# One transfer per load for a pair's keys and low-rank inputs, token rows of v stored by head, token rows of b and k by TensorE transposes

## The chip, the cores and the metric

The kernel runs on one core of one Trainium2 chip. The metric is device time in microseconds (us) of that core, from one launch; lower is better. The kernel before takes 3005.72 us, the median of 3 runs (3000.78 to 3016.42).

## What is computed

One layer of a hybrid diffusion backbone on 1024 latent tokens and 128 context tokens, with a model width of 1024, all in fp32. A combined input projection (`z = h @ w_in`) feeds a bidirectional RWKV-7 mixer of 16 heads x 64 and a gated short convolution. Both are projected, merged by gates and added to x. A gated MLP with a width-3 convolution follows. The part that the change touches is the RWKV-7 mixer:

```python
def step(s, inp):
    r_t, w_t, k_t, v_t, a_t, b_t = inp           # a = -kk, b = kk * a
    sa = jnp.einsum('bhij,bhj->bhi', s, a_t)
    s = s * w_t[:, :, None, :] + sa[..., None] * b_t[:, :, None, :] + v_t[..., None] * k_t[:, :, None, :]
    return s, jnp.einsum('bhij,bhj->bhi', s, r_t)
...
w_log = -softplus(-(decay_w0[d] + tanh(wdown) @ decay_w2[d])) - 0.5
decay = exp(-exp(w_log))
a = sigmoid(iclr_a0[d] + adown @ iclr_a2[d])
k_d = heads(k * (1.0 + (a - 1.0) * k_a))
y, s_fin = wkv_scan(s0, rh, heads(decay), k_d, vh, kk, heads(a), reverse)
```

It is run forward and backward over the tokens.

## The kernel before, in words

**Two kinds of work on TensorE.** `Kern.dense` (line 230) goes through a list of jobs, each one 128-column tile of a projection: 3 column blocks (`th`) of 384 tokens x 8 contraction tiles x 3 matmuls (fp32 split in a high and a low part). Into this stream, `step_streams` (line 151) weaves the mixer's own small matmuls. The weaving is planned in Python while the program is built: each instruction adds a cost in ns to a clock, a stream goes on when the clock has passed its due time `s.t` and its condition holds, and priorities are handed to the scheduler of the language below. TensorE, ScalarE, VectorE and the DMA queue of SyncE (SP) each work their instructions in order. `K.dma` (line 125) sends nearly all transfers to the SP queue; only `Xw` goes to ScalarE's and `Dm` to GpSimd's.

**Dense jobs of this part, in order** (lines 553 to 695): two low-rank inputs (`T_WD`, `T_AD`, written by `lora_evac` to the DRAM tiles `LO`), then k, r and v of pair 0 and of pair 1 (`rkv`), the gate input `T_GD`, the gate output `gjobs` (24 fp32 matmul tiles from `gts`, evacuated by `g_evac` on ScalarE and stored to `GS`), then `rkv` of the other pairs between the convolution's jobs, the 16 gate jobs, and the 8 jobs of `w_pb`. A pair is 2 heads (128 channels). `gts` are 3 tiles of the tag `rot`, which has 4 buffers; `k_evac` takes its tile `kt` from the same tag.

**Streams of the mixer** (class `Scan`, line 984):
- `prep` (line 1106), 24 times (8 pairs x 3 blocks): loads k, kk and r of the pair (3 transfers into `krk`), the low-rank inputs by `lora_in` (2 transfers into `llo`, 49 calls), and writes for both directions the features FA (a, r times decay) and FB (b and k over decay) to DRAM, one transfer each per segment.
- `features` and `prep2` (lines 1190, 1208), 36 items (4 groups of 2 pairs x 9 chunks of 128 tokens): load FA into `E` and `O` and FB into `BK` (one buffer), form the Gram matrices `gpb` and `gpk`, and turn b and k into token rows: for each of 8 blocks, 2 heads and b or k, one matmul of `BK` against the identity into `bps` (lines 1243 to 1246), 32 matmuls of 64x64 for an item.
- `vfill` (line 1252): brings the token rows of v into `Wt`, 4 transfers for each half of an item. The rows were made by `v_evac` (transposes `vps`, line 599) and stored to `VT[d]`.
- `chain`, `merge`, `scan`, `finish`: a triangular inverse on VectorE (31 steps), then the state recurrence on TensorE, then the normalisation and the store `oa`.

Of the kernel before, what the change touches and what calls it, by code (L numbers as in the profile page):

```python
# [15 lines left out]
P = 128  # L16
# [325 lines left out]
def build(tc, ins, outs, dbg=None):  # L342
# [4 lines left out]
    with es:  # L347
# [9 lines left out]
        dt_ = lambda name, shape=(P, T): dr.tile(list(shape), F32, name=name, tag=name)  # L357
        RS = [dt_(f"rs{m}") for m in range(8)]
        KS = [dt_(f"ks{m}") for m in range(8)]
        KKS = [dt_(f"kks{m}") for m in range(8)]  # L360
        VS = [dt_(f"vs{m}") for m in range(8)]
        LO = [dt_(f"lo{m}") for m in range(4)]
        FA = [dt_(f"fa{m}", (P, 2, 2, 2 * T)) for m in range(4)]
        FB = [dt_(f"fb{m}", (P, 2, 2, 2 * T)) for m in range(4)]
        BS = [dt_(f"bs{m}") for m in range(8)]
        VT = [dt_(f"vt{d}", (T, D)) for d in range(2)]
        GS = [dt_(f"gs{m}") for m in range(8)]
# [142 lines left out]
        with ExitStack() as ea:  # L510
# [16 lines left out]
            K.sc = Scan(K, const, apool, par, pc, mask, ident, bones, x0, hw0, hka, oka,  # L527
                        dict(RS=RS, KS=KS, KKS=KKS, VS=VS, LO=LO, GS=GS, OA=OA, FA=FA, FB=FB, BS=BS, VT=VT))
            hx = lambda k: (H[k][0], H[k][1])
# [9 lines left out]
            def lora_evac(base, func):  # L539
                def ev(s, th, ps):  # L540
                    sl = slice(th * TH, th * TH + TH)
                    z = st.tile([P, TH], F32, name="lz", tag="st")
                    K.act(s, z, ps, func)
                    hi = st.tile([P, TH], F32R, name="lh", tag="st")
                    lo = st.tile([P, TH], F32R, name="ll", tag="st")
                    K.act(s, hi, z, AF.Copy)
                    K.tt(s, lo, z, hi.bitcast(F32), ALU.subtract)
                    for d in range(2):
                        K.dma(LO[base + d][0:64, sl], hi[64 * d:64 * d + 64, :].bitcast(F32), "lo")
                        K.dma(LO[base + d][64:128, sl], lo[64 * d:64 * d + 64, :].bitcast(F32), "lo")  # L550
                return ev

            job(T_WD, lora_evac(0, AF.Tanh))
            job(T_AD, lora_evac(2, AF.Copy))

# [9 lines left out]
            def g_evac(s, m, th, ps):  # L565
                z = st.tile([P, TH], F32, name="gz", tag="st")
                K.act(s, z, ps, AF.Copy)
                K.dma(GS[m][:, th * TH:th * TH + TH], z, "gs")
# [13 lines left out]
            def v_evac(m):  # L582

                def ev(s, th, ps):
# [8 lines left out]
                    def post(s2):  # L593
                        t0, ms = th * TH, slice(m * P, m * P + P)
                        for d, zd in enumerate((z, zr)):
                            yield
                            pv = K.psd.tile([P, 512], F32, name="vps", tag="psd")
                            for j in range(3):
                                K.transp(pv[:, j * P:j * P + P], zd[:, j * P:j * P + P], ident, cost=110)
                            s2.t = clk.now  # L600
                            zt = st.tile([P, 3, P], F32, name="vt", tag="st")
                            K.act(s2, zt, pv[:, :TH].rearrange("p (j f) -> p j f", f=P), AF.Copy)
                            for a, b, _ in latctx(th):
                                r0 = t0 + a if d == 0 or t0 + a >= TL else TL - t0 - b
                                K.dma(VT[d][r0:r0 + b - a, ms].rearrange("(j t) f -> t j f", t=P),
                                      zt[:, a // P:b // P], "vt")
                        K.events.add(("v", m, th))
# [76 lines left out]

            rkv(0)
            rkv(1)
            job(T_GD, gd_evac)
            gjobs()
# [295 lines left out]
class Scan:  # L984
# [4 lines left out]
    def __init__(self, K, const, apool, par, pc, mask, ident, bones, x0, hw0, hka, oka, dr):  # L989
# [25 lines left out]
        self.W = self.one.tile([P, 2, 4, 2, C], F32, name="Wt", tag="Wt")  # L1015
        self.y, self.PC = {}, {}
        self.NY = 4

    def start(self):
# [4 lines left out]
        def prep_all(s):  # L1024
            yield lambda: ("kk", 0, 0) in ev and ("r", 0, 0) in ev
            self.lora_in(0, 0)
            for p in range(NPAIR):
                yield lambda: ("kk", p, 0) in ev and ("r", p, 0) in ev
                yield from self.lora_w(s, p)
                for th in (0, 2, 1):  # L1030
                    yield lambda: ("kk", p, th) in ev and ("r", p, th) in ev
                    yield from self.prep(s, p, th)
                    ev.add(("prep", p, th))

        def ready(i, what):
            pp, n = self.items[i]
            ths = {n // 3, (7 - n) // 3} if n < 8 else {2}
            return all((what, 2 * pp + q, th) in ev for q in range(2) for th in ths)

# [66 lines left out]
    def prep(self, s, p, th):  # L1106
# [6 lines left out]
        krk = self.one.tile([P, 3, TH], F32, name="krk", tag="krk")  # L1113
        for j, src in enumerate((dr["KS"], dr["KKS"], dr["RS"])):
            K.dma(krk[:, j, :], src[p][:, t0:t0 + TH], "ld")
        if pp not in self.PC:
# [5 lines left out]
        for d in range(2):  # L1122
# [52 lines left out]
            for a, b in segs:  # L1175
                g0 = t0 + a if d == 0 or t0 + a >= TL else TL - t0 - b
                K.act(s, PC[:, q, d, g0 // C:(g0 + b - a) // C], e65[:, a // C:b // C, C], AF.Copy)
                for dst, src in (("FA", FAo), ("FB", B)):
                    K.dma(dr[dst][pp][:, q, d, 2 * g0:2 * (g0 + b - a)],
                          src[:, a // C:b // C].rearrange("p c a t -> p (c a t)"), "fa")  # L1180
            yield

    def lora_in(self, th, d):

        llo = self.one.tile([P, 2, TH], F32R, name="llo", tag="llo")
        for w in range(2):
            self.K.dma(llo[:, w, :].bitcast(F32), self.dr["LO"][2 * w + d][:, th * TH:th * TH + TH], "llo")
        self.llo = llo, self.K.clk.now + 4000
# [19 lines left out]
    def prep2(self, s, i, pp, n):  # L1208
# [5 lines left out]
        for q in range(2):  # L1214
# [4 lines left out]
            for e in range(4 * q, 4 * q + 4):  # L1219
                for ps, a in ((gb, 1), (gk, 0)):  # L1220
                    for h in range(2):
                        o = HS[h if a else 1 - h]
                        calls.append(lambda ps=ps, a=a, h=h, e=e, o=o: K.mm(
                            ps[o, e - 4 * q, :], BK[HS[h], e, a, :], (E, O)[h][HS[h], e, :], True, True, 85))
            K.group(calls)
# [12 lines left out]
        for x in range(4):  # L1238
            for c in range(2):
# [3 lines left out]
        pv = [self.psm.tile([P, 512], F32, name="bps", tag="psm").rearrange("p (e t) -> p e t", t=C) for _ in range(2)]  # L1243
        K.group([lambda e=e, a=a, h=h: K.mm(pv[h][HS[h if a else 1 - h], e, :], BK[HS[h], e, a, :],
                                            self.ident[HS[h], HS[h]], True, True, 45)
                 for e in range(8)[::-1] for a in range(2) for h in range(2)])
        s.t = K.clk.now
# [4 lines left out]
    def vfill(self, s, i, pp, n):  # L1252
# [5 lines left out]
        for c in range(2):  # L1258
# [8 lines left out]
            ch = (2 * n + c if n < 8 else c) * C  # L1267
            for d in range(2):
                rows = self.dr["VT"][d][base + ch:base + ch + C, 256 * pp:256 * pp + 256]
                rows = rows.rearrange("t (q h f) -> t q h f", q=2, h=2)  # L1270
                for h in range(2):
                    K.dma(Wt[64 - 64 * h:128 - 64 * h, h, d::2, c, :], rows[:, :, h, :], "v")
            if c == 0 and n == 8:
# [259 lines left out]
```

## Time and profile before

| | us |
|---|---|
| median of 3 runs (lowest, highest) | 3005.72 (3000.78, 3016.42) |
| profiled execution, its own time | 2994.76 |
| its span, first to last instruction | 2993.0 |
| TensorE busy in the span | 2771.6 |
| VectorE busy | 2009.7 |
| ScalarE busy | 1266.4 |

The span is nearly all of the execution's time. PE is TensorE's matmul row, PEld its weight loads (which overlap the matmuls), DVE VectorE, ACT ScalarE, POOL GpSimd, SP the queue of SyncE that issues transfers. Matmuls are pipelined, so a busy PE is not a PE at its peak. "The granted clock" is the share of full speed that TensorE was given; in the rows it is either full or half, and a stretch's number is the mean. A name such as `psd<-gz,wraw` is the output tile and then the inputs.

### The profile page before, as it was taken

The page shows a single profiled execution, that of the slowest core. Times are in us where ns is not written, and L with a number is a line of the kernel's source. Part 1 is how long each engine was busy: PE and PEld are TensorE (multiplying, and loading weights), DVE is VectorE, ACT ScalarE, POOL GpSimd, SP SyncE. Part 2 cuts the span into 40 slices and gives each one's busy share as a digit, 9 for nine tenths or more (in the row PEclk, how much of TensorE's full clock was granted, in tenths as well). Part 3 has the DMA queues.
Part 4 walks back from the last instruction along what each step waited for, and adds up shares of the span by engine and source line. Part 5 has one row for each costly group of instructions (what it writes and reads, how often), then busy time and mean ns, then how long its engine had stood idle before and what let it go on. Part 6 is the DMA issues. An engine that isn't in the chain of part 4 may idle for free. (4 is left out here: it accounts for less than half of the span.)

```text
span 2993.0 us, 63336 instructions
## 1 busy us (share of the span) xinstructions
PE 2771.6 (93%) x24762; PEld 2514.2 (84%) x24762; DVE 2009.7 (67%) x5039; ACT 1266.4 (42%) x2540; POOL 318.9 (11%) x342
## 2 busy tenths in 40 slices
PE   7886989999989988988998999899999999999997
PEld 3774778878778877777777789899999999999996
DVE  8367666677568779989877865965555454454556
ACT  5464536454545633334543544023443241424243
POOL 3211111111111111111111112100000000000001
PEclk9997999999999999999999999999999999999999
DMA  4577646464655644544554538853211111111112
GB/s 191 179 240 204 197 121 209 145 180 143 184 172 166 197 118 127 136 115 122 148 136 120 137 101 279 291 165 98 68 43 36 50 40 45 41 41 43 41 44 81
DMA packets 425937, 388.50 MB, mean 130 GB/s; under 512 B 189477, under 2 KB 362405, under 8 KB 425637
## 3 DMA queue, kind: packets, MB, share of 16 engines
q1 hardware_dynamic: 379558, 360.84, 39.6%
q0 software_dynamic: 6912, 18.88, 2.3%
q10 hardware_dynamic: 39168, 4.73, 1.0%
q8 instruction: 195, 3.19, 0.5%
q14 instruction: 104, 0.85, 0.1%
HBM read 268.17 MB, written 116.13 MB: 128 GB/s over the span
## 5 line engine op out<-in xcount | busy, mean ns | idle before, releaser
L89 PE MATMUL psd<-h,whi 128*128 128x384 f32 x3216 | 909.3, 355 | 20.4 <-ACT h L105 9.3
L89 PEld LDWEIGHTS psd<-h,whi 128*128 128x128 f32 x3216 | 592.3, 192 | 58.6 <-issue 12.6
L89 PE MATMUL psd<-h,wlo 128*128 128x384 f32 x1608 | 564.5, 352 | 3.6 <-POOL wlo L110 3.6
L89 PE MATMUL psd<-g,whi 128*128 128x384 f32 (+1 forms) x2112 | 543.2, 338 | 0.0
L105 ACT ACTIVATE whi<-wraw 128x512 fp32r<-128x512 f32 (+2 forms) x334 | 198.4, 595 | 457.5 <-PE psd L89 358.6
L89 PEld LDWEIGHTS psd<-g,whi 128*128 128x128 f32 x2112 | 383.5, 188 | 0.3
L89 PE MATMUL psd<-g,wlo 128*128 128x384 f32 (+1 forms) x1056 | 355.9, 337 | 0.0
L110 POOL TENSOR_TENSOR wlo<-wraw,whi 128x512 fp32r<-128x512 f32 x148 | 207.1, 1402 | 1208.6 <-ACT whi L105 1057.4
L89 PEld LDWEIGHTS psd<-h,wlo 128*128 128x128 f32 x1608 | 309.3, 192 | 17.3 <-POOL wlo L110 5.2
L110 DVE TENSOR_TENSOR X<-X,Xt 128x60 f32<-128x60 f32 (+24 forms) x1116 | 258.0, 233 | 27.3
L110 DVE TENSOR_TENSOR Xt<-X,Dm 128x60 f32<-128x60 f32 (+24 forms) x1116 | 257.4, 233 | 27.0
L89 PE MATMUL psd<-a,whi 128*128 128x384 f32 x864 | 219.0, 334 | 0.0
L89 PE MATMUL psd<-x,whi 128*128 128x384 f32 x768 | 199.7, 341 | 8.0 <-ACT x L105 4.4
L89 PEld LDWEIGHTS psd<-g,wlo 128*128 128x128 f32 x1056 | 199.3, 189 | 0.0
L110 DVE TENSOR_TENSOR wlo<-wraw,whi 128x512 fp32r<-128x512 f32 (+2 forms) x186 | 113.7, 612 | 102.9 <-ACT whi L105 102.9
L89 PEld LDWEIGHTS psd<-a,whi 128*128 128x128 f32 x864 | 156.0, 188 | 0.0
L110 DVE TENSOR_TENSOR fu<-psd,rs 128x384 f32<-128x384 f32 x132 | 73.4, 556 | 117.3 <-PE psd L89 105.2
L89 PEld LDWEIGHTS psd<-x,whi 128*128 128x128 f32 x768 | 140.6, 191 | 10.3 <-ACT x L105 4.7
L89 PE MATMUL psd<-a,wlo 128*128 128x384 f32 x432 | 144.0, 334 | 0.0
L122 DVE SCALAR_TENSOR_TENSOR x<-psd,mod,x 128x384 f32<-128x384 f32 (+3 forms) x160 | 79.2, 515 | 93.9 <-PE psd L89 93.8
L105 ACT ACTIVATE BK<-BK,PC 128x128 f32<-128x128 f32 x288 | 93.2, 392 | 102.2 <-PE gpk L89 77.9
L89 PE MATMUL psd<-x,wlo 128*128 128x384 f32 x384 | 130.5, 340 | 5.4 <-DVE wlo L110 5.4
(206 smaller groups left out, 4917.7 us busy)
## 6 DMA issues: line engine op xcount, KB each, us to landing
wraw<-in_w_in SPq DMA_DIRECT2D x134, 256.0 KB, 3.2
wraw<-in_w_up SPq DMA_DIRECT2D x88, 256.0 KB, 2.6
llo<-lo SPq DMA_DIRECT2D x98, 192.0 KB, 2.7
BK<-fb SPq DMA_DIRECT2D x36, 512.0 KB, 4.8
Dm<-Dd POOLq DMA_DIRECT2D x144, 128.0 KB, 3.6
wx<-in_wmb SPq DMA_DIRECT2D x32, 512.0 KB, 5.3
fa<-fa SPq DMA_DIRECT2D x40, 384.0 KB, 2.7
fb<-ak SPq DMA_DIRECT2D x40, 384.0 KB, 3.0
```

The costliest lines, as they stand in the source:

```text
L89: return self.nc.tensor.matmul(out, lhsT=lhsT, rhs=rhs, start=start, stop=stop)
L105: self.nc.scalar.activation(out, in_, func, bias=bias, scale=scale)
L110: e.tensor_tensor(out, a, b, op)
L122: self.nc.vector.scalar_tensor_tensor(out, a, sc, b, op0, op1)
```

## The change

1. `RS`, `KS`, `KKS` become slices of one DRAM tile `KR[m]` of 128 x 3 x 1152, and `prep` loads all three in one transfer. `LO` becomes 2 tiles of 128 x 2 x 1152, and `lora_in` loads both parts in one.
2. `VT` becomes one tile laid out token, group, head, (pair, direction), feature. The stores of v's token rows are made by head (2 where there was 1, in pieces of 256 bytes, which were 512), and `vfill` loads by head (2 transfers for a half of an item, which were 4).
3. FB is stored in three transfers where there was one: the upper 64 partitions as they are, the lower 64 with b and k exchanged. With that order, `prep2` makes the token rows by 16 transposes of 64x128 where it made 32 matmuls, and the Gram matmuls pick their operand accordingly.
4. An item's loads may be planned only when 5000 ns of the planner's clock have passed since its prep ended (`made`).
5. The job `T_GD` moves ahead of `rkv(1)`; `g_evac` alternates between ScalarE and VectorE.

```diff
-        RS = [dt_(f"rs{m}") for m in range(8)]
-        KS = [dt_(f"ks{m}") for m in range(8)]
-        KKS = [dt_(f"kks{m}") for m in range(8)]
+        KR = [dt_(f"kr{m}", (P, 3, T)) for m in range(8)]
+        KS, KKS, RS = [[kr[:, j] for kr in KR] for j in range(3)]
...
-        LO = [dt_(f"lo{m}") for m in range(4)]
+        LO = [dt_(f"lo{d}", (P, 2, T)) for d in range(2)]
...
-        VT = [dt_(f"vt{d}", (T, D)) for d in range(2)]
+        VT = dt_("vt", (T, 4, 2, 4, HD))
...
-                z = st.tile([P, TH], F32, name="gz", tag="st")
-                K.act(s, z, ps, AF.Copy)
+                z = st.tile([P, TH], F32, name="gs", tag="st")
+                if (m + th) % 2:
+                    K.act(s, z, ps, AF.Copy)
+                else:
+                    nc.vector.tensor_copy(z, ps)
+                    s.use("V", 530)
...
-                                K.dma(VT[d][r0:r0 + b - a, ms].rearrange("(j t) f -> t j f", t=P),
-                                      zt[:, a // P:b // P], "vt")
+                                for h in range(2):
+                                    K.dma(VT[r0:r0 + b - a, m // 2, h, 2 * (m % 2) + d].rearrange("(j t) f -> t j f", t=P),
+                                          zt[:, a // P:b // P, h * HD:h * HD + HD], "vt")
...
             rkv(0)
+            job(T_GD, gd_evac)
             rkv(1)
-            job(T_GD, gd_evac)
             gjobs()
...
-                    ev.add(("prep", p, th))
+                    self.made[p, th] = K.clk.now + 5000
...
-        for j, src in enumerate((dr["KS"], dr["KKS"], dr["RS"])):
-            K.dma(krk[:, j, :], src[p][:, t0:t0 + TH], "ld")
+        K.dma(krk, dr["KR"][p][:, :, t0:t0 + TH], "ld")
...
-                for dst, src in (("FA", FAo), ("FB", B)):
-                    K.dma(dr[dst][pp][:, q, d, 2 * g0:2 * (g0 + b - a)],
-                          src[:, a // C:b // C].rearrange("p c a t -> p (c a t)"), "fa")
+                cols = slice(2 * g0, 2 * (g0 + b - a))
+                K.dma(dr["FA"][pp][:, q, d, cols], FAo[:, a // C:b // C].rearrange("p c a t -> p (c a t)"), "fa")
+
+                K.dma(dr["FB"][pp][64:128, q, d, cols], B[64:128, a // C:b // C].rearrange("p c a t -> p (c a t)"), "fb")
+                for j in range(2):
+                    K.dma(dr["FB"][pp][0:64, q, d, cols].rearrange("p (c a t) -> p c a t", a=2, t=C)[:, :, j, :],
+                          B[0:64, a // C:b // C, 1 - j, :], "fb")
...
-        for w in range(2):
-            self.K.dma(llo[:, w, :].bitcast(F32), self.dr["LO"][2 * w + d][:, th * TH:th * TH + TH], "llo")
+        self.K.dma(llo.bitcast(F32), self.dr["LO"][d][:, :, th * TH:th * TH + TH], "llo")
...
-                            ps[o, e - 4 * q, :], BK[HS[h], e, a, :], (E, O)[h][HS[h], e, :], True, True, 85))
+                            ps[o, e - 4 * q, :], BK[HS[h], e, a if h else 1 - a, :], (E, O)[h][HS[h], e, :], True, True, 85))
...
-        K.group([lambda e=e, a=a, h=h: K.mm(pv[h][HS[h if a else 1 - h], e, :], BK[HS[h], e, a, :],
-                                            self.ident[HS[h], HS[h]], True, True, 45)
-                 for e in range(8)[::-1] for a in range(2) for h in range(2)])
+        K.group([lambda e=e, h=h: K.transp(pv[h][:, e, :], BK[HS[h], e].rearrange("p a t -> p (a t)"),
+                                           self.ident[HS[h], HS[h]], cost=40)
+                 for e in range(8)[::-1] for h in range(2)])
...
-            for d in range(2):
-                rows = self.dr["VT"][d][base + ch:base + ch + C, 256 * pp:256 * pp + 256]
-                rows = rows.rearrange("t (q h f) -> t q h f", q=2, h=2)
-                for h in range(2):
-                    K.dma(Wt[64 - 64 * h:128 - 64 * h, h, d::2, c, :], rows[:, :, h, :], "v")
+            for h in range(2):
+                K.dma(Wt[64 - 64 * h:128 - 64 * h, h, :, c, :], self.dr["VT"][base + ch:base + ch + C, pp, h], "v")
```

## Rows read from the trace of the kernel before

**Rows 1.** The page: busy us, share of the span, instructions of each engine
```profile
PE 2771.6 (93%) x24762; PEld 2514.2 (84%) x24762; DVE 2009.7 (67%) x5039; ACT 1266.4 (42%) x2540; POOL 318.9 (11%) x342
```
**Rows 2.** Stretches: length; busy of PE, PEld, DVE, ACT, POOL; granted clock; DMA share; GB/s
```profile
217.00:298.00 81.00, 46.59 (x418) 30.43 (x417) 58.98 (x194) 37.39 (x90) 8.54 (x14) 0.70 0.70 208
298.00:1050.00 752.00, 690.63 (x6551) 608.32 (x6551) 516.57 (x1296) 386.35 (x831) 115.71 (x109) 0.96 0.57 172
1050.00:1800.00 750.00, 689.63 (x10373) 580.75 (x10372) 619.50 (x2202) 308.72 (x690) 106.51 (x144) 0.98 0.48 126
1800.00:1936.00 136.00, 122.69 (x683) 119.90 (x681) 107.30 (x175) 39.02 (x77) 26.89 (x17) 0.97 0.86 290
```
**Rows 3.** Tiles oa and pbz: ns min/median/max, first and last start, us
```profile
L128 SPq DMA_DIRECT2D oa<-fg x40: 319/385/1612, 647.7 to 1801.6; - x40
L122 DVE SCALAR_TENSOR_TENSOR pbz<-pbz,psd x24: 541/548/555, 1835.7 to 1937.0; 128x384 f32<-128x384 f32 x24
```
**Rows 4.** Tile bps: its matmuls; then sums over the 100-us stretches 100 to 1800
```profile
L89 PE MATMUL bps<-ident,BK x2304: 218/218/366, 236.9 to 1721.2; 64*64 64x64 f32 x192
...
sum 1700.00, PE 82.10 PEld 67.12 ACT 40.54; mean PE 4.83 PEld 3.95 ACT 2.38
```
**Rows 5.** Timeline of PE: start, us, instruction; a whole item, a broken one, v's transposes
```profile
254.26 1.16 PE L89 MATMUL bps<-ident,BK 64*64 64x64 f32 x64
...
1573.53 1.16 PE L89 MATMUL bps<-ident,BK 64*64 64x64 f32 x23
1574.45 0.37 PE L89 MATMUL px<-SX,G 64*64 64x64 f32 x2
...
1578.00 0.40 PE L89 MATMUL bps<-ident,BK 64*64 64x64 f32 x10
...
138.97 0.49 PE L100 MATMUL vps<-ident,vz 128*128 128x128 f32 x3
```
**Rows 6.** Waits of PE from 217 to 298: total us, times, longest
```profile
PE gpb L89 <- DMA BK<-fb: 9.8, 2, 8.1
PE psd L89 <- ACT gz L105: 7.5, 3, 3.5
PE psd L89 <- DMA wraw<-in_g: 6.9, 1, 6.9
PE gpb L89 <- DMA gs<-gz: 5.6, 1, 5.6
```
**Rows 7.** Tile gz and timeline of ACT: evacuations and stores of the g jobs
```profile
L128 SPq DMA_DIRECT2D gs<-gz x24: 319/382/1422, 242.9 to 299.0; - x24
...
262.65 0.49 ACT L105 ACTIVATE gz<-psd 128x384 f32<-128x384 f32 x1 [6.09 <-DMA gs<-gz]
...
281.35 1.02 ACT L105 ACTIVATE gz<-psd 128x384 f32<-128x384 f32 x2 [5.26 <-DVE X L110]
```
**Rows 8.** Timeline of SP: k and kk of one block of pair 1 stored
```profile
158.10 0.38 SPq L128 DMA_DIRECT2D ks<-kt  x1
...
166.09 0.36 SPq L128 DMA_DIRECT2D kks<-kr  x1
```
**Rows 9.** Tiles: issue time on SP, ns min/median/max, first and last start
```profile
L128 SPq DMA_DIRECT2D Wt<-vt x288: 573/596/1652, 194.2 to 1760.9; - x144
L128 SPq DMA_DIRECT2D vt<-vt x64: 360/427/1736, 140.0 to 1051.4; - x64
L128 SPq DMA_DIRECT2D krk<-ks x24: 319/423/768, 112.7 to 1027.7; - x24
L128 SPq DMA_DIRECT2D llo<-lo x98: 319/424/1794, 87.5 to 1037.9; - x98
L128 SPq DMA_DIRECT2D fb<-ak x56: 319/338/919, 131.8 to 1051.9; - x56
L128 SPq DMA_DIRECT2D E<-fa x36: 527/568/1811, 221.7 to 1695.2; - x36
```
**Rows 10.** Waits of PE from 298 to 1050
```profile
PE fps L89 <- DMA fb<-bs: 6.0, 3, 2.6
...
PE lps L89 <- DMA llo<-lo: 5.0, 3, 2.5
PE gpb L89 <- DMA BK<-fb: 4.3, 2, 3.5
```
**Rows 11.** Stretch with tile vps alone: PE, PEld, ACT; granted clock; DMA share
```profile
100.00:217.00 117.00, 6.11 (x36) 4.29 (x36) 5.62 (x12) 0.99 0.69 224
```

More of the change, by code (lines that the diff above doesn't have):

```diff
@@ L527, in build @@
             K.sc = Scan(K, const, apool, par, pc, mask, ident, bones, x0, hw0, hka, oka,
-                        dict(RS=RS, KS=KS, KKS=KKS, VS=VS, LO=LO, GS=GS, OA=OA, FA=FA, FB=FB, BS=BS, VT=VT))
+                        dict(KR=KR, VS=VS, LO=LO, GS=GS, OA=OA, FA=FA, FB=FB, BS=BS, VT=VT))
             hx = lambda k: (H[k][0], H[k][1])
@@ L548, in ev @@
                     for d in range(2):
-                        K.dma(LO[base + d][0:64, sl], hi[64 * d:64 * d + 64, :].bitcast(F32), "lo")
-                        K.dma(LO[base + d][64:128, sl], lo[64 * d:64 * d + 64, :].bitcast(F32), "lo")
+                        K.dma(LO[d][0:64, base, sl], hi[64 * d:64 * d + 64, :].bitcast(F32), "lo")
+                        K.dma(LO[d][64:128, base, sl], lo[64 * d:64 * d + 64, :].bitcast(F32), "lo")
                 return ev
             job(T_WD, lora_evac(0, AF.Tanh))
-            job(T_AD, lora_evac(2, AF.Copy))
+            job(T_AD, lora_evac(1, AF.Copy))
             gts = []
@@ L593, in post @@
                     def post(s2):
-                        t0, ms = th * TH, slice(m * P, m * P + P)
+                        t0 = th * TH
                         for d, zd in enumerate((z, zr)):
@@ L1015, in __init__ @@
         self.W = self.one.tile([P, 2, 4, 2, C], F32, name="Wt", tag="Wt")
-        self.y, self.PC = {}, {}
+        self.y, self.PC, self.made = {}, {}, {}
         self.NY = 4
@@ L1037, in ready @@
             ths = {n // 3, (7 - n) // 3} if n < 8 else {2}
-            return all((what, 2 * pp + q, th) in ev for q in range(2) for th in ths)
+            keys = [(2 * pp + q, th) for q in range(2) for th in ths]
+            if what == "prep":
+                return all(self.made.get(k, 1e12) <= K.clk.now for k in keys)
+            return all((what, *k) in ev for k in keys)
         def prep2_all(s):
```

## The prediction

> **What bounds the kernel now.** I read the page first, then the busy times by stretch, then the tiles at the seam of the stages, and last the waits of PE in each stretch. PE is busy for 2771.6 of 2993.0 us [rows 1]. In the two long stretches of the mixer it is busy 690.63 of 752 and 689.63 of 750 us [rows 2], so about 120 us are idle there, with dense work always waiting behind. What sets the end is seen at the seam: the mixer's last store of `oa` is issued at 1801.6, but the `w_pb` jobs, the tail of the same dense list, go on until 1937.0 [rows 3]. The scan is done more than 100 us before the dense list. So a microsecond that PE no longer spends or waits before 1800 brings the end forward, and a scan that runs later, but not by 100 us, costs nothing. VectorE's 619.50 of 750 us [rows 2] is high, but it holds up the scan, not the dense list, as long as the list fills PE.
>
> One stretch is far worse than the others: from 217 to 298 PE is busy for 46.59 of 81 us at a mean granted clock of 0.70 [rows 2]. There the g jobs and the first scan items meet.
>
> **Token rows of b and k by transposes.** Now 2304 matmul instructions (36 items x 32 matmuls x 2 passes), 82.10 us of PE busy [rows 4], so 82.10 / 36 = 2.28 us an item. An unbroken item takes 1.16 us [rows 5]: four 64x64 quadrants go side by side, (1.16 - 0.22) / 15 = 0.06 us for each four. The other 1.12 us is the price of being broken up by other matmuls, as in the item that goes from 1573.53 to 1578.40 in pieces [rows 5]. After, 16 transposes, one instruction each, as v's three blocks are three instructions. Those follow each other at (0.49 - 0.27) / 2 = 0.11 us with 128 weight columns [rows 5], which the new ones have too, though they move 64 columns and use half the rows. The kernel before has no such shape, so I bound it. Single file: 15 x 0.11 + 0.27 = 1.92, plus all of the breaking-up, 3.04 an item: (3.04 - 2.28) x 36 = 27 us lost. Two heads side by side at the quadrants' step: 7 x 0.06 + 0.22 = 0.64 and nothing broken: 59 us won. I take two heads side by side, as the quadrants do, at the 0.11 of the row with the same weight columns: 7 x 0.11 + 0.27 = 1.04, and half of the breaking-up since a quarter of the instructions offers fewer places for it: 1.60. That is 0.68 x 36 = 24 us of PE. Some pieces of `bps` lie where `px` would otherwise wait, so I count three quarters: **18 us won**.
>
> A passage of the Trainium skill speaks against this part: TensorE: Matmul & The Clock Gate, Part 4, says that transposes do not count as PE activity for the clock. Rows speak first: 36 of v's transposes lie in a stretch whose granted clock is 0.99 [rows 11]. There they are thin among dense matmuls, as the new ones will be, so I give the passage a small chance, as a rival below.
>
> **T_GD ahead of rkv(1), and g's evacuation on two engines.** The lost time of the stretch is 81 - 46.59 = 34 us idle, and some 0.30 x 46.59 = 14 us of work is due to the half clock: 48 us. Its waits are named [rows 6]: 6.9 for the g weights, 9.8 for `BK`, 7.5 for the evacuation of g, and 5.6 behind g's stores. They are linked. The first g store is issued only at 242.9, as SP stands at other transfers, so the buffers run out and ACT waits 6.09 us for a store; later ACT stands 5.26 us behind a transfer that it issues for the chain on DVE [rows 7]. Afterwards the gate input is ready a whole `rkv` earlier, half of the evacuations pass by DVE (12 x 0.53 us by the planner's number in the diff, on an engine idle for 22 of the 81 us [rows 2]), and `made` moves the first items' loads, which crowd SP there, back by 5 us. None of this removes the meeting of the g jobs and the first items for certain. Ends: all but 3 of the 48 us won; or a loss, since the three `gts` now hold three of the four `rot` buffers while pair 1's three `kt` go through the fourth. One `kt` is held from the k store to the kk store, 166.09 - 158.10 = 8 us [rows 8], against 24 matmuls of 122.69 / 683 = 0.18 us, the step of the nearly all dense stretch [rows 2], so 4 us, for a block of the dense job; two hand-overs late by 4 and 8 us, 12 at worst. The three banks of `psd` hide part of that. I take half of the 48: **24 us won**, between 45 won and 12 lost. What is late next there is the prep of pair 1, later by one dense job, with 100 us to spare at the far end.
>
> **Transfers.** SP loses 48 issues for `krk` at 0.42 and 49 for `llo` at 0.42 (41 us), and 144 of `Wt` at 0.60 (86 us). The `Wt` issues that stay have four pieces a row in place of two, as `E` has at 0.57 against 0.60 [rows 9], so no dearer. It gains 64 `vt` at 0.43 (27 us) and, for FB, 56 x (3 issues of 0.34 to 0.60, less the 0.34 of now): 38 to 82 us. In all 18 to 62 us less issue time. But the additions all lie before 1052, while the `Wt` savings spread to 1761 [rows 9]: before 1050 at most (1050 - 194) / (1761 - 194) = 55% of 86, 47 us, are saved, so there SP goes from 23 us less to 21 us more. PE's waits for these loads from 298 to 1050 are 5.0 (`llo`) and 4.3 (`BK`), and 6.0 for one that changes only by its place in the queue [rows 10]: 15 us can be won or, if they double, lost. I take **0**. An SP instruction of FB that waits for VectorE holds the next `llo` and the weights behind it; lower-partition stores now wait at the same place, not at a new one. The planner's clock runs 36 x (32 x 45 - 16 x 40) ns = 29 us shorter, which shifts the weave; its sign is open, 10 us either way.
>
> **Sum.** 18 + 24 + 0 = 42 us off 2994.76 gives 2953 for an execution like the profiled one. The median of the runs lies 11 us above the profiled execution; I carry that over: **2964**.
>
> **The rivals.**
> 1. *More than that.* The transposes pack at the quadrants' step and the stretch clears: 45 + 40 = 85 us, 2921. For it: the waits of rows 6 have one root. Against it: nothing shows the packing for half the rows and all columns.
> 2. *Off the path.* The transposes only lay bare waits on ACT and DVE, and the g jobs meet the first items one job later just the same: 0 to 15 us, 2991 to 3006. For it: unbroken, 1.04 against 1.16 us is hardly anything, and DVE's load in 1050 to 1800.
> 3. *Slower: SP comes to set the pace of prep.* Each of the 56 segments puts up to 1.5 us more issue ahead of the loads that PE's next low-rank matmul needs, and the one load of k, kk and r can't start before the last of three stores to one tile. If PE feels it in full, 82 + 27 - 41 - 47 = 21 us, the waits of rows 10 double (15), and pair 1's `kt` costs its 12 us; with 18 won at the transposes and nothing in the stretch: 30 us more, 3036. It decides once PE waits for `llo` in more than a few of the 48 passes (3 now).
> 4. *Slower by the clock.* If each item's transposes dropped the clock, say from the mean of 0.97 to 0.90 over the 1500 us of both stretches [rows 2], 0.07 x 1500 = 105 us would go: about 3070 with the other gains. The passage cited above would bring it about; rows 11 are against it.
>
> That the transposes don't take place as one instruction each is ruled out by rows 5.
>
> **How the numbers follow.** A measurement of this kernel tells about 0.5% (15 us) from no change: faster is below 2991, slower above 3021. Forecast (2940 to 2988) 0.54; more than that 0.14; off the path 0.16; SP 0.11; clock 0.05. Faster: 0.54 + 0.14 and a little of the off-path case, 0.69; same 0.15; slower 0.16. The range that leaves out the two slower cases and the far end of the first is 2920 to 3008.
>
> **What would show it.** Each step has its line: `bps` with 576 matmuls and under 60 us busy where it had 82.10 (over 82: single file); the stores of g spread over under 40 us where 56 lie between the first and the last [rows 7], PE idle under 20 us there and the granted clock above 0.85; `llo` and `BK` waits of PE from 298 to 1050 near 9 us (twice that: rival 3); the granted clock of the long stretches near 0.97 (0.90: rival 4). The forecast is wrong if the stores of g still stretch over 50 us, or if PE's idle time grows by what `bps` gives up.

## The result, and the profile after

The changed kernel takes 3087.82 us (median of 4 runs, 3083.72 to 3093.72) where the kernel before took 3005.40 in the runs beside it: a ratio of 1.027, 95% interval 1.0236 to 1.0304, **slower by about 82 us**. The forecast was 2964, and its range ended at 3008.

The page of the changed kernel: the span, then busy us, share and instructions of PE (before: [rows 1]).

```profile
span 3089.2 us, 59833 instructions
...
PE 2795.0 (90%) x23034; PEld 2532.1 (82%) x23034; DVE 2007.1 (65%) x5051; ACT 1264.0 (41%) x2525; POOL 310.5 (10%) x342
```

PE has 1728 instructions less, as meant, and yet is busy for 23 us more; the other 73 us of the longer span are idle time (294.2 us for 221.4). The stretches of the changed kernel, with the columns of [rows 2] and answering to its first three lines:

```profile
217.00:298.00 81.00, 43.73 (x290) 34.73 (x289) 42.88 (x87) 41.66 (x93) 2.77 (x5) 0.69 0.70 194
298.00:1050.00 752.00, 640.32 (x5481) 559.61 (x5480) 499.80 (x1307) 352.57 (x746) 105.45 (x108) 0.91 0.57 160
1050.00:1800.00 750.00, 678.97 (x8674) 570.65 (x8673) 586.19 (x2020) 298.20 (x691) 106.84 (x140) 0.92 0.50 131
```

From 298 to 1050 PE is idle for 112 us where it was 61, and its granted clock is 0.91 where it was 0.96. After 1050 the idle time is hardly more (71 for 60), but the clock is 0.92 for 0.98, so the same work holds PE longer. Idle time and half clock together are the loss; what the transposes save lies within it. PE busy in `bps` alone, 217 to 1900 (before: 82.10, [rows 4]):

```profile
217.00:1900.00 1683.00, 47.90 (x576) 36.54 (x576) 40.36 (x72) 0.91 0.54 146
```

What PE waits for, 100 to 1190, in the kernel before (total us, times, longest):

```profile
PE gpb L89 <- DMA BK<-fb: 14.1, 4, 8.1
...
PE lps L89 <- DMA llo<-lo: 8.4, 6, 2.5
...
PE gpb L89 <- DMA E<-fa: 0.3, 1, 0.3
```

and in the changed kernel:

```profile
PE gpb L89 <- DMA E<-fa: 39.8, 5, 14.5
PE gpb L89 <- DMA BK<-fb: 27.0, 3, 16.5
PE lps L89 <- DMA llo<-lo: 16.4, 9, 6.7
PE fps L89 <- DMA fb<-bs: 12.4, 3, 6.0
```

The first matmuls of an item (`gpb`) wait for `E` and `BK`, which are loaded from what prep has stored in FA and FB. Prep is late, and the row that says so is the one of its stores of FB, in the tile `fb` (issue time, ns min/median/max; first and last start, us):

```profile
L128 SPq DMA_DIRECT2D fb<-ak x168: 473/606/1762, 132.5 to 1144.4; - x168
```

Before there were 56 issues of 338 ns, the last at 1051.9 [rows 9]. Now 168 issues of 606 ns, and the last comes 92.5 us later. One step of prep on SP, start and length in us:

```profile
275.57 1.83 SPq L128 DMA_DIRECT2D fb<-ak  x3
277.44 1.57 SPq L128 DMA_DIRECT2D lwraw<-in_lw  x2
279.11 0.57 SPq L128 DMA_DIRECT2D BK<-fb  x1
```

and the matmul on PE that had waited for this `BK`, idle for 16.48 us before it:

```profile
286.53 0.44 PE L89 MATMUL gpb<-E,BK 64*64 64x128 f32 x1 [16.48 <-DMA BK<-fb]
```

The seam of the stages moved as a whole. The last store of `oa`, then the last product of `w_pb`, in the changed kernel ([rows 3] before: 1801.6 and 1937.0):

```profile
L128 SPq DMA_DIRECT2D oa<-fg x40: 319/408/1772, 727.0 to 1937.8; - x40
```
```profile
L122 DVE SCALAR_TENSOR_TENSOR pbz<-pbz,psd x24: 542/548/555, 1931.9 to 2033.1; 128x384 f32<-128x384 f32 x24
```

The scan is still done 95 us before the dense list, so the list, and PE's lost time in it, sets the end as before.

### The profile page after: what moved, and what is told of

It is laid out like the page before. It is cut to its first block, busy times and chain, and to the rows that moved or that the text cites. A ratio compares the mean times of both kernels' runs of the same rounds, so it can differ in the third digit from the quotient of the medians.

```text
span 3089.2 us, 59833 instructions
## 1 busy us (share of the span) xinstructions
PE 2795.0 (90%) x23034; PEld 2532.1 (82%) x23034; DVE 2007.1 (65%) x5051; ACT 1264.0 (41%) x2525; POOL 310.5 (10%) x342
## 4 chain that ended last, share of the span: by engine, by line
PE 62%; DVE 21%; DMA 8%; ACT 3%; issue 3%; SPq 2%; POOL 0%; ACTq 0%; DVEq 0%; POOLq 0%
PE psd L89 48%; DVE X L110 4%; DVE Xt L110 4%; PE px L89 3%; SPq L128 2%; PE mps L89 2%; PE py L89 1%; PE gpb L89 1%; DVE ak L110 1%; PE fps L89 1%; PE bps L100 1%; PE lps L89 1%; PE gpk L89 1%; DMA llo<-lo 1%; DMA krk<-kr 1%
## 5 line engine op out<-in xcount | busy, mean ns | idle before, releaser
L89 PE MATMUL psd<-h,whi 128*128 128x384 f32 x3216 | 925.0, 360 | 27.7 <-ACT whi L105 12.3
L89 PEld LDWEIGHTS psd<-h,whi 128*128 128x128 f32 x3216 | 602.8, 196 | 65.9 <-ACT whi L105 14.8
L89 PE MATMUL psd<-h,wlo 128*128 128x384 f32 x1608 | 571.1, 356 | 6.0 <-POOL wlo L110 6.0
L89 PEld LDWEIGHTS psd<-h,wlo 128*128 128x128 f32 x1608 | 315.5, 196 | 21.2 <-POOL wlo L110 9.5
L110 POOL TENSOR_TENSOR wlo<-wraw,whi 128x512 fp32r<-128x512 f32 x148 | 199.1, 1349 | 1256.3 <-ACT whi L105 1051.6
L89 PE MATMUL gpb<-E,BK 64*64 64x128 f32 x576 | 92.7, 306 | 75.7 <-DMA E<-fa 40.8
L89 PEld LDWEIGHTS gpb<-E,BK 64*64 64x64 f32 x576 | 67.8, 148 | 90.8 <-issue 75.6
```

Of the source, the lines that this page charges most:

```text
L89: return self.nc.tensor.matmul(out, lhsT=lhsT, rhs=rhs, start=start, stop=stop)
L110: e.tensor_tensor(out, a, b, op)
```

## Experiments

Five theories of the loss stood at the outset. S: the three FB stores hold up prep. C: the clock falls with the transposes. O: the new order, with the gate's projection ahead of `rkv(1)`. W: the planner's clock (`made`, and an item's transposes at 640 ns for the matmuls' 1440) places the work badly. E: the combined transfers wait longer. Experiments on the kernel before have labels in b_, those on the changed kernel in a_. Each ratio is to the kernel before in the runs beside it, with its 95% interval.

**Each part alone, on the kernel before.** T_GD and g:

```
-            rkv(1)
             job(T_GD, gd_evac)
+            rkv(1)
...
+                if (m + th) % 2: K.act(s, z, ps, AF.Copy)
+                else: nc.vector.tensor_copy(z, ps)
```


> The kernel before with one part alone: the gate's input projection (T_GD) ahead of the second rkv, and the evacuations of the gate alternating between ScalarE and VectorE. Theory O (the new order is the culprit: the three gate tiles hold three of the four rot buffers while k tiles of rkv(1) wait for the fourth): slower by 30 us or more, since the changed kernel had lost 37 us by its 1800th dense matmul. Theory S (the three-way FB stores set the pace of prep), theory C (the clock falls with the transposes) and theory W (the planner's clock places the work of an item too late): no loss here, 24 us won as predicted, at least between 12 us lost and 45 won.

Measured: 2990.50 us, 0.995 (0.9931 to 0.9969). O falls: alone, this part loses nothing. But its reason isn't borne out either. The stores of g, and PE from 217 to 298:

```profile
L128 SPq DMA_DIRECT2D gs<-gs x24: 319/376/1222, 234.8 to 301.8; - x24
```
```profile
217.00:298.00 81.00, 47.05 (x449) 31.83 (x448) 57.09 (x182) 34.66 (x83) 7.25 (x13) 0.75 0.73 214
```

The stores stretch over 67 us (56 in [rows 7]) and PE is as idle there as before.

The delay of the loads:

```
-                    ev.add(("prep", p, th))
+                    self.made[p, th] = K.clk.now + 5000
```


> The kernel before with one part alone: an item's loads are planned 5 us of the planner's clock after the prep that they need. Theory W: slower by 30 to 60 us, because every item of the prep stage comes later, with long waits for BK and E near the items' start. Theories O, S and C: within 10 us of the kernel before, as the prediction had it.

Measured: 2994.86 us, 0.9964 (0.9943 to 0.9986). No loss.

FB in three stores with the transposes:

```
+                K.dma(FB[64:128, ...], B[64:128, ...])
+                for j in range(2):
+                    K.dma(FB[0:64, ...][:, :, j, :], B[0:64, ..., 1 - j, :])
...
-        32 x K.mm(pv[h][...], BK[HS[h], e, a, :], ident, ..., 45)
+        16 x K.transp(pv[h][:, e, :], BK[HS[h], e], ident, cost=40)
```


> The kernel before with one part alone: FB stored in three pieces with the halves of head 0 swapped, and 16 transposes for 32 matmuls per item. Theory S: slower by 50 to 90 us, with PE's wait for E<-fa up from 7.4 us to over 30. Theory C: slower by 30 to 60 us with a granted clock near 0.92 in 1050 to 1800 (0.98 before), E<-fa waits as before. Theories O and W: 18 us won as predicted (the planner's cost of an item falls from 1440 to 640 ns here too, so W may take some of it back).

Measured: 3006.58 us, 1.0002 (0.9985 to 1.002). Its stores of FB, and two of PE's waits from 100 to 1190:

```profile
L128 SPq DMA_DIRECT2D fb<-ak x168: 451/598/1563, 132.2 to 1114.1; - x168
```
```profile
PE gpb L89 <- DMA BK<-fb: 21.4, 3, 19.6
PE gpb L89 <- DMA E<-fa: 14.1, 5, 7.1
```

Prep ends 62 us later and the waits have grown, yet no time is lost by the part as a whole.

The combined transfers:

```
+        K.dma(krk, KR[p][:, :, t0:t0 + TH])      # for three
+        self.K.dma(llo, LO[d][:, :, ...])        # for two
+            for h in range(2): K.dma(Wt[...], VT[..., pp, h])   # for four
```


> The kernel before with one part alone: k, kk and r of a pair in one DRAM tile read by one transfer, the low-rank inputs likewise, the token rows of v by head (stores doubled, reads halved). The prediction had 0, within 15 us. Theory E (one transfer for three waits for the last of the three and lands later, and the stores of v by head hold SyncE): slower by 20 us or more, with longer waits of lps for llo (8.4 us before) and px for Wt (0.9). Theories S, O, C and W: within 10 us.

Measured: 3010.33 us, 1.0016 (0.9994 to 1.0038): no loss that can be told. Its `llo` waits of 100 to 1190 are 11.5 us in 10 (8.4 in 6 before), and its last FB store is issued at 1081.8, 30 us later than before. So no part alone explains 82 us: they lose together.

**Each part taken back, from the changed kernel.** First T_GD and g:

> The changed kernel with the gate's projection and evacuations put back as before (the other parts stay). The four parts alone gave 0.995, 0.996, 1.000 and 1.002 of the time of before, so their sum would be near 2982 us, and the loss of 82 us comes from parts together. If the gate's place is one of them: 3010 us or less. If not: 3080 to 3110.

Measured: 3063.07 us, 1.0193 (1.0162 to 1.0225).

> The changed kernel without the delay of 5 us on the planner's clock between a prep and the loads that need it. If the delay is one of the parts that lose together (theory W: FB's later stores and the later loads place the item badly): 3010 us or less. If not: 3080 to 3110.

Measured: 3082.56 us, 1.0259 (1.0228 to 1.029).

> The changed kernel with FB in one store and the 32 matmuls as before. If the stores or the transposes (theories S and C) are one of the parts that lose together: 3010 us or less, E<-fa waits in prep back under 15 us (39.8 in the changed kernel). If not: 3080 to 3110.

Measured: 3012.36 us, 1.002 (1.0001 to 1.0039).

> The changed kernel with the transfers of k, kk and r, of the low-rank inputs and of v as before. If the combined transfers are one of the parts that lose together (theory E: a load that waits for the last of three, more stores of v on SyncE ahead of FB's): 3010 us or less. If not: 3080 to 3110.

Measured: 3047.36 us, 1.0145 (1.0104 to 1.0186).

Only without the FB part does nearly all of the loss go; `made` matters little; the combined transfers and the gate's place give back 40 and 25 us. Both of the latter results missed the two values expected and lie between. In the kernel without the FB part the stores and waits are back:

```profile
L128 SPq DMA_DIRECT2D fb<-ak x56: 319/336/2022, 133.0 to 1062.8; - x56
```
```profile
PE gpb L89 <- DMA BK<-fb: 5.6, 4, 2.5
...
PE gpb L89 <- DMA E<-fa: 3.0, 3, 1.4
```

**The halves of the FB part, inside the changed kernel.** The transposes as matmuls of the same shape (`K.mm` for `K.transp`, all else kept):

> The changed kernel with each of the 16 transposes of an item written as a plain matmul of the same shape against the identity: the same stores, layouts and planner's costs. Theory C (the granted clock falls because a transpose counts for less than a matmul): the time at half clock falls from 350 us towards 160, the span by about half of that, to 3000 to 3015 us. Theory S (the three-way stores) and theory W (the planner's cost of 640 ns for 1440): within 15 us of the changed kernel, 3072 to 3103.

Measured: 3138.31 us, 1.045 (1.0417 to 1.0483): 50 us slower than with the transposes, which no theory had. An item, in two pieces:

```profile
1670.65 1.77 PE L89 MATMUL bps<-ident,BK 64*128 64x64 f32 x26
...
1672.96 0.66 PE L89 MATMUL bps<-ident,BK 64*128 64x64 f32 x6
```

1.77 + 0.66 = 2.4 us for 32 instructions (16 products in two passes), against 1.16 for 64 instructions of 64 columns, spread over the four quadrants [rows 5]. In 217 to 1900 `bps` is busy for 122.53 us, more than the 82.10 of before. That the clock is 0.93 in 1050 to 1800 here too, without a transpose in `bps`, speaks against C:

```profile
1050.00:1800.00 750.00, 688.75 (x8911) 588.33 (x8911) 582.72 (x2026) 290.00 (x671) 100.55 (x135) 0.93 0.48 126
```

The three stores with the 32 small matmuls:

> The changed kernel with the three FB stores kept and the 32 matmuls of 64 columns of before, at their planner's cost of 1440 ns. Theory S: 3070 us or more, E<-fa waits over 30 us. Theories C and W: 3000 to 3025.

Measured: 3056.51 us, 1.0173 (1.0144 to 1.0203), 44 us above the kernel without the FB part. Its stores of FB, PE's waits from 100 to 1190, and the two long stretches:

```profile
L128 SPq DMA_DIRECT2D fb<-ak x168: 466/607/1522, 132.9 to 1154.0; - x168
```
```profile
PE gpb L89 <- DMA E<-fa: 32.6, 5, 15.2
PE gpb L89 <- DMA BK<-fb: 21.7, 3, 14.4
```
```profile
298.00:1050.00 752.00, 645.24 (x5973) 568.40 (x5974) 498.69 (x1301) 350.10 (x748) 108.17 (x109) 0.92 0.57 161
1050.00:1800.00 750.00, 689.76 (x10211) 582.38 (x10205) 624.69 (x2155) 318.22 (x728) 111.17 (x148) 0.99 0.52 136
```

So **the stores lose without the transposes too**. From 298 to 1050 the clock is 0.92 with no transpose in `bps` and PE idle for 107 us. From 1050 to 1800 it is 0.99, where the changed kernel has 0.92: the stores alone don't bring that about.

The transposes at the planner's cost of the matmuls (`cost=90` for `cost=40`):

> The changed kernel with the transposes at the planner's cost of the matmuls that they replace (90 ns each, 1440 ns per item; 640 in the changed kernel). Theory W: 3000 to 3025 us. Theories C and S: 3070 or more.

Measured: 3087.05 us, 1.027 (1.0247 to 1.0294), the changed kernel's own time. The planner's cost of an item isn't what loses: W falls for this difference. With this cost the transposes can be held against the matmuls of the run before: beside three stores they make the kernel 31 us slower (3087.05 for 3056.51).

One FB store, 8 transposes and 16 small matmuls in turn:

```
+        for e in ...: for a in range(2): K.mm(pv[0][HS[1 - a], e, :], BK[HS[0], e, a, :], ...)
+                      K.transp(pv[1][:, e, :], BK[HS[1], e], ...)
```


> The changed kernel with FB stored in one piece as before; 8 transposes of an item for the second head, 16 matmuls for the first, planner's cost 1440 ns. Theory S: 3000 to 3015 us, as without the FB part (3012). Theory C: between that and the changed kernel, some 3040 to 3055, with 220 to 270 us at half clock. Theory W: near 3012.

Measured: 3083.37 us, 1.0258 (1.0233 to 1.0283), with the last FB store at 1063.6. This kernel loses elsewhere than the others, from 1050 to 1800:

```profile
1050.00:1800.00 750.00, 707.15 (x8796) 582.22 (x8793) 562.09 (x1989) 262.59 (x612) 98.85 (x136) 0.88 0.45 116
```

PE is hardly idle and the granted clock is only 0.88. The timeline of one item there:

```profile
1521.28 0.33 PE L89 MATMUL bps<-ident,BK 64*64 64x64 f32 x4
1521.54 0.27 PE L100 MATMUL bps<-ident,BK 64*128 64x64 f32 x1
1521.74 0.33 PE L89 MATMUL bps<-ident,BK 64*64 64x64 f32 x4
```

Each four small matmuls and one transpose take 0.46 us; in 217 to 1900 `bps` is busy for 130.50 us against 82.10 and 47.90. So this kernel doesn't tell stores from transposes: the alternation has a cost of its own. The next one has none.

**Pure transposes with one store.** The halves of head 0 change places when ScalarE copies them out of PSUM:

```
+        K.act(s, BT[:, 1], pv[1], AF.Copy)
+        for a in range(2):
+            K.act(s, BT[HS[1 - a], 0], pv[0][HS[a]], AF.Copy)
```


> The changed kernel with FB in one store as before and all 16 transposes of an item kept (the halves of head 0 change places when the product is copied out of PSUM, one more short ScalarE copy per item). If the three FB stores are the main loss (45 us with the matmuls kept) and pure transposes save PE time: 2985 to 3015 us, E<-fa waits of 100 to 1190 under 15. If transposes lose by themselves (theory C, or the mix with 64-column matmuls): 3060 or more, with a clock under 0.94 in 1050 to 1800.

Measured: **2998.37 us**, 0.9969 (0.9952 to 0.9985), 90 us under the changed kernel. Its stretches, one unbroken item, and its FB stores:

```profile
298.00:1050.00 752.00, 667.34 (x5727) 587.36 (x5726) 514.26 (x1339) 373.56 (x796) 113.98 (x110) 0.95 0.57 167
1050.00:1800.00 750.00, 696.92 (x9397) 582.60 (x9395) 631.34 (x2232) 333.24 (x743) 110.21 (x149) 0.97 0.52 133
```
```profile
1472.28 0.72 PE L100 MATMUL bps<-ident,BK 64*128 64x64 f32 x16
```
```profile
L128 SPq DMA_DIRECT2D fb<-ak x56: 319/332/1081, 133.4 to 1085.8; - x56
```

576 transposes, and a clock of 0.95 and 0.97, where the kernel with matmuls and one store has 0.97 in both: **C falls for transposes that stand together, beside one store.** They take 0.72 us an item for 1.16. The time is 14 us under that of the kernel with matmuls and one store (3012.36), where the prediction had 18; but the planner's cost differs there too, and below an order alone moves more than that.

**What of the three stores costs.** On ScalarE's queue instead of SyncE's (`fb="A"` in `QUEUE`):

> The changed kernel with the three FB stores issued by ScalarE's queue in place of SyncE's, same pieces and bytes. If the loss is SyncE's order (two more issues of 0.6 us and the wait for the last product stand ahead of the next loads): 3020 to 3050 us, E<-fa waits under 20. If it is the pieces of 256 bytes themselves, or the place where the planner puts the loads: 3075 or more.

Measured: 3074.06 us, 1.0235 (1.0195 to 1.0275). PE's waits for `E` are gone from its list and those for `BK` are 1.5 us (39.8 and 27.0 in the changed kernel), but the time hardly falls, and the last FB store is still issued at 1138.9. This doesn't clear SyncE's order: the issues now stand among ScalarE's own instructions, and PE waits longer for these. Its waits for `thw`, a tile of prep that ScalarE writes, are 9.8 us in 5 in the changed kernel (100 to 1190), and here

```profile
PE lps L89 <- ACT thw L105: 23.8, 11, 6.6
```

The tile `ak`, its stores, then for what ScalarE sat idle before its instructions on `ak` (us, times):

```profile
L128 ACTq DMA_DIRECT2D fb<-ak x168: 476/616/2321, 132.1 to 1138.9; - x168
...
  DMA fb<-ak: 26.0, 21
```

`ak` has one buffer. 21 times ScalarE, coming to write the next `ak`, stood until the stores of the last one had landed. But with the stores on SyncE this wait doesn't grow with their number. The kernel with one store and 2998 us, then the changed kernel with three (the kernel before: 5.6 us in 6):

```profile
  DMA fb<-ak: 15.3, 11
```
```profile
  DMA fb<-ak: 16.0, 10
```

So ScalarE's wait for the one buffer doesn't account for the loss.

The same number of stores without short pieces, from the kernel with 2998 us:

```
+                for r in (slice(64, 128), slice(0, 32), slice(32, 64)):
+                    K.dma(FB[pp][r, q, d, cols], B[r, ...])
```


> The changed kernel with one-piece layout of FB (the halves change places when copied out of PSUM, 2998 us with one store), its store cut into three by rows: 64, 32 and 32 partitions in long pieces, no piece of 256 bytes. From the first to the last of the three issues passes time in which the chain of prep cannot go on, since its one buffer is still being read; over 48 steps that was 23 to 27 us with one store and 107 to 116 with three. If this is the cause (the number of issues per step): 3045 to 3090 us, prep's last store after 1110 us. If it is the pieces of 256 bytes, or the halves' order in FB: 2985 to 3015.

Measured: 3072.58 us, 1.0217 (1.0173 to 1.0262), 74 us more than with one store.

```profile
L128 SPq DMA_DIRECT2D fb<-ak x168: 317/486/1277, 132.6 to 1143.3; - x168
...
  DMA fb<-ak: 11.6, 8
```

**It is, for the most part, the number of stores in the step, not their pieces of 256 bytes nor the order of the halves.** The expectation's reason, the one buffer, isn't borne out: ScalarE waits 11.6 us for it, less than with one store. By the rows, 168 issues of 606 ns against 56 of 338 are 101.8 and 18.9 us, so the stores of the 48 steps of prep (24 times, two directions) take SyncE 83 us longer to issue in the changed kernel, and 63 us longer here. Prep's last store comes 92.5 us later in the changed kernel than in the kernel before, and here 57.5 us later than with one store (1085.8).

**How much an order alone can do.** The kernel before with 20 for 45 in the planner's cost of its 32 matmuls, no instruction changed:

> The kernel before, with the planner told 20 ns for each of the 32 matmuls of an item in place of 45 (640 ns per item as in the changed kernel): the same instructions in another order. If the order alone moves the time, by 10 us or more either way. If the losses all come from operations and transfers: 2998 to 3010.

Measured: 2983.06 us, 0.9922 (0.9898 to 0.9946). The same work in another order is some 24 us faster (1 - 0.9922 of 3007.71). So a difference of 15 us between two kernels here can't be put down to the part that differs.

**The parts that are worth keeping.** On the kernel before: the gate's part, `made`, and the pure transposes with one FB store, first at the planner's cost of 90 each:

> The kernel before with the gate's projection early and its evacuations on both engines (0.995 alone), the delay of 5 us (0.996 alone), and 16 transposes per item with one FB store. If the three add up and the transposes win the 18 us of the prediction: 2950 to 2970 us. If the parts don't add (order): 2985 to 3010. If transposes lose by themselves: 3010 or more.

Measured: 2976.59 us, 0.9905 (0.987 to 0.9939). Then at 40:

> The kernel before with the gate's projection early, the delay of 5 us, 16 transposes with one FB store, and the planner's cost of an item at 640 ns (1440 in the same kernel that gave 0.9905). If the order's gain of 640 ns seen alone (0.992) adds: 2955 to 2970 us. If an order's gain belongs to its own kernel only: 2965 to 3000.

Measured: **2958.47 us, 0.9831 (0.9798 to 0.9863)**, faster than both kernels. Its span and PE, and two stretches:

```profile
span 2947.8 us, 59937 instructions
...
PE 2745.3 (93%) x23034; PEld 2487.6 (84%) x23034; DVE 2006.9 (68%) x5051; ACT 1285.1 (44%) x2563; POOL 314.4 (11%) x342
```
```profile
298.00:1050.00 752.00, 685.02 (x6280) 603.06 (x6280) 542.33 (x1377) 399.77 (x859) 115.10 (x113) 0.96 0.58 175
1050.00:1800.00 750.00, 703.04 (x9193) 591.95 (x9192) 620.07 (x2184) 332.07 (x728) 111.42 (x145) 0.97 0.51 133
```

The last FB store is issued at 1032.9, the earliest of all the kernels, and PE is busy for 26 us less than in the kernel before. The two kernels differ only in the planner's cost, and so in order, and lie 18 us apart; how much of the gain belongs to which part isn't shown.

## Why the prediction was wrong

**What bounds the kernel** was right: the dense list sets the end, and the scan keeps 95 us of room.

**The transposes** were right in kind and too small in PE time: 82.10 to 47.90 us are 34 us of PE where 24 were reckoned, as an unbroken item takes 0.72 us and not 1.04. At the end 18 us were put down. Beside one store the kernel with transposes is 14 us faster, which an order alone can make; beside three stores it is 31 us slower at the same planner's cost.

**The transfers were the step that failed**, the term that was put at 0. The prediction added up SyncE's issue time, FB's additions (38 to 82 us) against the savings of `krk`, `llo` and `Wt`, and came to 0 within 15 us. The size of FB's additions was right at its upper end: 83 us by the rows after. What was wrong is that they were set off at all. The savings brought nothing: alone, the combined transfers gave 1.0016, and in the changed kernel they cost 40 us (3047.36 without them). The additions stand in a step of prep that runs 48 times; in the changed kernel they cost 90 us (2998.37 with one store), and 74 without the short pieces. The sentence that the stores of the lower partitions "now wait at the same place, not at a new one" shows the error: it asks what waits on SyncE, and not who waits for what prep stores. PE waited 66.8 us for `E` and `BK`, where it had been 14.4. Part by part, on the kernel before, a term of 0 would have held; it is beside the other parts that the stores lose.

**Rival 3** named the place, SyncE's three issues ahead of the loads of prep, but took the same difference, 82 + 27 - 41 - 47 = 21 us, and so ended at 3036. Its sign, `llo` and `BK` waits of PE of some 18 us from 298 to 1050, did not come: they are 7.3 us there. What came are waits for `E`, for which no term of the prediction stood:

```profile
PE gpb L89 <- DMA E<-fa: 25.3, 4, 13.3
...
PE gpb L89 <- DMA BK<-fb: 4.1, 1, 4.1
...
PE lps L89 <- DMA llo<-lo: 3.2, 4, 1.7
```

Whether SyncE's order is the link from the stores to the loss stays open: from ScalarE's queue the stores lose nearly as much, but there they hold ScalarE.

**Rival 4** had its sign (0.91 and 0.92 in the long stretches) without its cause: with the same 576 transposes and one store the clock is 0.95 and 0.97. In the first stretch three stores without transposes bring it to 0.92. In the second they leave it at 0.99; there it is low only with three stores and transposes together (0.92, and 0.96 at the planner's cost of 90) or with the 64x128 matmuls (0.93), and on the kernel before it is 0.98 even with three stores and transposes. Why is open; as the kernels with 0.92 and 0.96 take the same time, the row by itself doesn't price the loss. The passage of the Trainium skill that the prediction cites (TensorE: Matmul & The Clock Gate, Part 4) would have the transposes lower the clock; beside one store, no run here shows it for transposes that stand together (0.97 from 1050 to 1800, as with matmuls). The sign couldn't tell the rivals apart, since the three stores bring the same row in the first stretch.

**T_GD and g's evacuations** were to bring 24 us by clearing the stretch from 217 to 298. Alone they brought 15, but the stretch did not clear: the stores of g still stretch over 67 us, which the prediction itself named as a mark against it. With 24 us from an order alone the 15 can't be called theirs. In the changed kernel they stretch over 55.5 us, with PE idle for 37 us at a clock of 0.69, and without the part that kernel is 25 us faster (3063.07), about what an order alone moves. The stores of g there:

```profile
L128 SPq DMA_DIRECT2D gs<-gs x24: 320/383/1054, 281.1 to 336.6; - x24
```

So the 24 us did not come either.

**The weave** was put at 10 us either way; the planner's lower cost alone gave 24 on the kernel before, and nothing in the changed kernel (3087.82 for 3087.05). That term was less than half of what it should have been.

What stays open: the same three stores lose 44 us beside matmuls, 74 to 90 beside transposes, and on the kernel before none that can be told, though prep's last store is late in all of them (1154.0, 1143.3 and 1144.4, 1114.1). The combined transfers make prep 30 us later by themselves, and 62 + 30 is the 92 of the changed kernel; that would fit if prep had some 60 us of room and no more. But the changed kernel without the combined transfers issues its last FB store at 1116.6, only 2.5 us after the kernel that lost nothing, and is 1.4% slower than the kernel before. So why the parts lose together isn't shown. Nor is the link from the stores to the loss: ScalarE's wait for the one buffer of `ak` is as short with one store as with three, and a kernel with two buffers was not tried; SyncE's order was tried only by giving the stores to ScalarE, which they then hold.

## What to carry to other kernels

A transfer more is not priced by setting its queue's time off against issues saved elsewhere: look at which step it stands in, how often that step runs, and who waits for its end. Here three issues for one in a step that runs 48 times cost 44 to 90 us in the changed kernel, and 241 issues saved elsewhere gave nothing back. Where an order is planned by a clock that knows nothing of transfers, change its costs alone once, to see how wide the scatter is, before a gain of a per cent is put down to an edit.

## What the runs showed of the hardware

- Sixteen fp32 transposes of 64x128 take 0.72 us, the same products as plain matmuls of 64x128 about 2.4 (in two pieces), as 64x64 matmuls in four quadrants 1.16. That a transpose should not be a plain matmul is also what the Trainium skill says (Perfetto Trace Analysis, Transposes); the 1.16 shows that small quadrants come closer than the wide matmul.
- Transposes and small matmuls in turn take 0.46 us for four and one: 130.50 / 36 = 3.6 us of PE busy an item, where the matmuls alone take 82.10 / 36 = 2.3 and the transposes alone 47.90 / 36 = 1.3; and the granted clock fell to 0.88 in a stretch in which PE was busy for 707 of 750 us.
- A store of part of a tile is no cheaper to issue than one of the whole: FB's three with short pieces took 606 ns each at the median, three of 64 and 32 partitions in long pieces 486, the whole tile in one 338.
